# A two-layer backbone step on one core: the second layer's modulation vectors made at other places, the sums joined with x two groups earlier, some work moved off VectorE at layer edges

## The chip, the cores and the metric

One core of a Trainium2 chip runs the whole program. The time is the device time of one execution in microseconds; the figure for a kernel is the median of several executions. The kernel before took 3270.18 us, the median of 3 runs (3263.32 to 3278.54).

## The reference, cut to what matters

Two layers run over 1152 tokens (1024 latent, 128 context) of width 1024. Latent and context tokens have a conditioning vector each, so that every modulation vector exists in two columns.

```python
def ada_modulation(cond, w_mod, b_mod):
    m = (jax.nn.silu(cond) @ w_mod + b_mod)[..., None, :]
    return jnp.split(m, 6, axis=-1)

def trunk_layer(x, cond, p, rg_h0, hg_s0, ctx_k, ctx_v):
    sh1, sc1, g1, sh2, sc2, g2 = ada_modulation(cond, p['w_mod'], p['b_mod'])
    h = rms_norm(x, p['norm1']) * (1 + sc1) + sh1
    xa, ga, bq, bff, bfb, bi, bg, cq, ck, cv = jnp.split(h @ p['w_in'], split_points, axis=-1)
    ...   # three mixers: convolution and RG-LRU, HGRN2, attention
    mix = jnp.concatenate([out_a, out_b, out_c.reshape(bsz, t_len, D_C)], axis=-1) @ p['w_out']
    x = x + g1 * mix
    h2 = rms_norm(x, p['norm2']) * (1 + sc2) + sh2
    x = x + g2 * (jnp.square(jax.nn.relu(h2 @ p['w1'])) @ p['w2'])
```

A layer's modulation is 6 × 1024 values for each of the two conditionings: 48 tiles of 128 values, numbered j = 0 to 47 in the order sh1, sc1, g1, sh2, sc2, g2.

## The kernel before, in words

Features lie on partitions, tokens along the free axis: 8 tiles of 128 features by 1152 tokens. A layer passes through these stages, one after the other in TensorE's queue with some overlap: the input projections; the mixers, in which RG-LRU and HGRN2 (mostly VectorE) are woven with the remaining projections, and attention with the output projection; the first MLP product with w1; the second with w2. In the trace's order of time, the first layer's mixers run from about 117 to 790 us, its first MLP product from 800 to 1229, its second from 1235 to 1677; the second layer's mixers from 1758 to 2398, its MLP products from 2408 to 2833 and from 2838 to 3247.

All large matmuls are done in three passes on a high part and a low part of each operand. The high part is a rounded copy (ScalarE, L186), the low part the difference, made by GpSimd (`psub`, L189) or VectorE (`vsub`, L192). Which engine takes which of a weight's seven low parts is `lo_subs`, with the counts in `W2_SUBS`.

Both MLP products run by a scheme that needs seven products of operand sums in place of eight (`Line.products`, L1105): a product is one set of seven, with banks bA, bB, bC and bE of PSUM. It has 84 matmuls of 288 columns in the first MLP product (32 products) and 42 in the second (64 products: 8 groups of 8). Its results are taken off the banks by `c11`, `c22`, `c12`, `c21` on ScalarE and VectorE. In the first MLP product these results are hidden units; they and their sums and differences are prepared as operands of the second and stored to memory: `od` holds those with a high and a low part, `or` the raw sums. Their places on chip are `od_` (2 places) and `hx_` (3), cut out of `spare`, which in the first layer is the tile `sil` that held the conditioning.

In the second MLP product, each group of products loads its operands into a ring of 18 tiles (`R`, pools `tp0` and `tp1`) and adds its results to `rows` (L198). `combine` (L1819) joins two rows at a time with x: rows = rows × g2 + x, at the places in `MERGE`; groups after that add with g2 as a scalar (L210). In the last group the squares of finished rows are summed (`Sums`), and rms_rest turns the sums into the next norm's scale: st (matmul), rr (VectorE, GpSimd), dg (a copy on VectorE, L183), rb (matmul), rs (ScalarE).

`mod_tile` (L276) makes one tile j of the modulation: pieces of w_mod are loaded (`wm`) and multiplied and summed with the conditioning `sil` by VectorE (L286), once for each conditioning. In the first layer, tiles 16 to 47 of its own modulation are made in the mixers (`mods`, L1447), in pieces of 384, 384 and 256. In the second MLP product of the first layer tiles 0 to 39 of the second layer's modulation are made in whole tiles of 1024 on the ring `hr_`, and in the second layer's second MLP product tiles 40 to 47 (`MODS2`). Small rings: `sqt` has four tiles of 384, `xt` 24, `g_` 28.

The instructions of each engine are put in a fixed order by a scheduler when the program is built; `high_priority` moves a piece forward. All DMAs are issued from SP's queue, in order, each behind the waits of those before it.

## Time and profile before

| | |
|---|---|
| runs, median (lowest, highest) | 3270.18 us (3263.32, 3278.54) |
| profiled execution, device time | 3276.47 us |
| its span, first to last instruction | 3274.7 us |
| mean granted TensorE clock | 0.95 |
| busy: TensorE, VectorE, ScalarE, GpSimd | 90%, 73%, 50%, 48% |
| moved by DMA | 566 MB, 173 GB/s on average |

Engines are called PE (TensorE), DVE (VectorE), ACT (ScalarE), POOL (GpSimd) and SP in the rows. PEclk is the granted share of TensorE's clock: 1.00 is 2.4 GHz, 0.50 is 1.2 GHz, and a mean between them is a share of the stretch at either. A busy share is an average over a stretch, so rows of one stage are set beside rows of the same stage in the other layer.

### The profile page before, as it was taken

What the parts mean: (1) busy time and instruction counts of PE and PEld (TensorE: products, weight loads), DVE (VectorE), ACT (ScalarE), POOL (GpSimd) and SP (SyncE); (2) the same over time, 40 slices, a digit from 0 to 9 for tenths busy, and PEclk for the clock granted to TensorE, in tenths of its full rate; (3) what the DMA queues carried; (4) which work ended last, traced back from release to release, by engine and by line L of the source; (5) the groups of instructions that cost most, each with busy time, mean ns of one, the idle gap of its engine ahead of it and who ended that gap; (6) DMA issues with size and microseconds to landing.
All of it is one profiled execution on the core that took longest, in us unless ns stands there. A gap on an engine that the chain in (4) does not pass through costs nothing. (4 is left out here: it accounts for less than half of the span.)

```text
span 3274.7 us, 61327 instructions
## 1 busy us (share of the span) xinstructions
PE 2960.4 (90%) x21208; PEld 2815.3 (86%) x21208; DVE 2406.1 (73%) x5283; ACT 1641.4 (50%) x4079; POOL 1567.8 (48%) x1528
## 2 busy tenths in 40 slices
PE   7888998998889998988868999999987999899995
PEld 7878888798789998888858889988977999899994
DVE  8899974667885568998874677346779755777787
ACT  5543234565566666344454533345646566654443
POOL 4541132345676665554545311334556765654453
PEclk8989999999899998999979999999998999999997
DMA  7342447983455567675522102689634655855552
GB/s 270 91 108 87 132 121 224 283 269 103 158 176 185 177 212 279 216 245 198 181 94 74 58 29 80 183 239 293 220 127 148 194 179 181 281 204 173 185 194 68
DMA packets 391318, 566.48 MB, mean 173 GB/s; under 512 B 45920, under 2 KB 250848, under 8 KB 391008
## 3 DMA queue, kind: packets, MB, share of 16 engines
q1 hardware_dynamic: 391008, 562.57, 53.8%
q8 instruction: 167, 2.74, 0.4%
q14 instruction: 143, 1.17, 0.1%
HBM read 397.01 MB, written 165.42 MB: 172 GB/s over the span
## 5 line engine op out<-in xcount | busy, mean ns | idle before, releaser
L189 POOL TENSOR_TENSOR wl<-wr,wh 128x512 fp32r<-128x512 f32 x164 | 231.1, 1413 | 485.4 <-ACT wh L186 379.2
L189 POOL TENSOR_TENSOR wt<-wl,wt 128x256 fp32r<-128x256 f32 x276 | 258.0, 942 | 176.5 <-ACT wt L186 116.5
L1110 PE MATMUL bB<-R,wt 128*128 128x288 f32 x768 | 236.9, 309 | 63.7 <-ACT bB L186 40.8
L189 POOL TENSOR_TENSOR ws<-wl,ws 128x512 fp32r<-128x512 f32 x160 | 227.5, 1426 | 121.4 <-ACT ws L186 121.3
L421 PE MATMUL pj<-hh,wh 128*128 128x384 f32 x640 | 223.7, 354 | 27.0 <-ACT g L213 12.3
L1110 PE MATMUL bB<-t,ws 128*128 128x288 f32 x768 | 231.7, 302 | 18.0 <-DVE hr L198 9.6
L423 PE MATMUL pj<-hh,wl 128*128 128x384 f32 x640 | 225.1, 352 | 7.1 <-POOL wl L189 7.1
L1111 PE MATMUL bB<-R,wt 128*128 128x288 f32 x768 | 231.1, 301 | 0.0
L1112 PE MATMUL bB<-R,wt 128*128 128x288 f32 x768 | 230.0, 300 | 0.0
L1111 PE MATMUL bB<-t,ws 128*128 128x288 f32 x768 | 229.6, 299 | 0.0
L1112 PE MATMUL bB<-t,ws 128*128 128x288 f32 x768 | 229.2, 299 | 0.0
L422 PE MATMUL pj<-hh,wh 128*128 128x384 f32 x640 | 223.4, 350 | 0.0
L1110 PEld LDWEIGHTS bB<-R,wt 128*128 128x128 f32 x768 | 148.2, 193 | 74.2 <-ACT bB L186 48.3
L186 ACT CAST wt<-wl 128x256 fp32r<-128x256 f32 x288 | 115.9, 406 | 159.8 <-PE bB L1112 82.0
L421 PE MATMUL wo<-u,wh 128*128 128x288 f32 x512 | 160.1, 314 | 17.1 <-DVE x L210 13.4
L1110 PEld LDWEIGHTS bB<-t,ws 128*128 128x128 f32 x768 | 147.6, 192 | 22.0 <-DVE hr L198 11.4
L186 ACT CAST wh<-wr 128x512 fp32r<-128x512 f32 x164 | 101.1, 618 | 129.3 <-PE pj L422 65.2
L207 POOL TENSOR_SCALAR pl<-pl,rc 128x384 f32<-128x384 f32 x128 | 79.1, 618 | 176.5 <-DVE rc L952 83.9
L1110 PE MATMUL bA<-R,wt 128*128 128x288 f32 x512 | 156.0, 305 | 8.1 <-DVE row L210 5.8
L1112 PE MATMUL bA<-t,ws 128*128 128x288 f32 x512 | 155.4, 304 | 8.0 <-DVE ws L192 6.5
L1110 PE MATMUL bA<-t,ws 128*128 128x288 f32 x512 | 155.1, 303 | 4.3 <-ACT ws L186 2.3
L1111 PE MATMUL bA<-R,wt 128*128 128x288 f32 x512 | 154.6, 302 | 0.0
(363 smaller groups left out, 11364.9 us busy)
## 6 DMA issues: line engine op xcount, KB each, us to landing
wr<-in_w SPq DMA_DIRECT2D x304, 256.0 KB, 3.3
R<-od SPq DMA_DIRECT2D x96, 576.0 KB, 5.6
xb<-or SPq DMA_DIRECT2D x128, 288.0 KB, 4.2
wm<-in_w_mod SPq DMA_DIRECT2D x64, 512.0 KB, 5.6
od<-sil SPq DMA_DIRECT2D x96, 288.0 KB, 2.9
od<-pad SPq DMA_DIRECT2D x96, 288.0 KB, 3.1
wr<-in_w_in SPq DMA_DIRECT2D x104, 256.0 KB, 3.0
bi<-in_bias SPq DMA_DIRECT2D x96, 192.0 KB, 4.5
```

The source lines that it names most:

```text
L186: nc.scalar.copy(out=out, in_=in_)
L189: nc.gpsimd.tensor_tensor(out=out, in0=a, in1=b, op=ALU.subtract)
L207: nc.gpsimd.tensor_scalar(out=out, in0=a, scalar1=s1, scalar2=s2, op0=op0, op1=op1)
L421: mm(ps, lhsT=wh(k), rhs=ah(k), start=k == first, stop=False)
L422: mm(ps, lhsT=wh(k), rhs=al(k), start=False, stop=False)
L423: mm(ps, lhsT=wl(k), rhs=ah(k), start=False, stop=k == last)
L1110: mm(ps, lhsT=w[:, 0, ti(i)], rhs=t[:, 0], start=start and i == 0, stop=False, skip_group_check=True)
L1111: mm(ps, lhsT=w[:, 0, ti(i)], rhs=t[:, 1], start=False, stop=False, skip_group_check=True)
L1112: mm(ps, lhsT=w[:, 1, ti(i)], rhs=t[:, 0], start=False, stop=i == n - 1, skip_group_check=True)
```

## The change

- **Modulation.** Tiles 0 to 15 of the second layer's modulation are made in the first layer's first MLP product, over products 10 to 30 (`MLP_MODS`), in pieces on `sqt`; tiles 16 to 47 in the second layer's mixers, by the loop that the first layer has had. The second MLP products make none. For this, `sil` is loaded again in the first MLP product, and from product 8 on `od_` and `hx_` come from the rings `xr_` and `sqt`. `sil2` then stays until the second layer's mixers end; RG-LRU's weights `gw` and the gates `gel` change pools in that layer.
- **Joins.** `MERGE` names places two groups earlier, so the last two groups add with g2 as a scalar.
- **Operand ring.** The 18 tiles come from three pools of 4, 11 and 3 in turn, where they came from two of 7 and 11 with the first three turns skipped.
- **Less on VectorE at edges.** The squares of the second half's x are summed as each output tile is done (`late`), not after all; the scale's second step (`rms_turn`) is put in without the first step's priority. The first chunk's low parts of the second layer are made by ScalarE and GpSimd (`spare_vector`); the 64 context columns of the MLP's norm go from VectorE to ScalarE; in the last group of the second MLP product GpSimd makes all low parts of the weights.

```diff
-MODS2 = (2, 44)
+MLP_MODS = (10, 30)
...
-MERGE = (NG - 2, 2, 0), (NG - 2, 3, 0), (NG - 1, 0, 0), (NG - 1, 1, 0)
+MERGE = (NG - 3, 2, 0), (NG - 3, 3, 0), (NG - 2, 0, 0), (NG - 2, 1, 0)
...
-            vts(u, u, g[:, 1:2], sh[:, 1:2])
+            act(u, u, AF.Identity, scale=g[:, 1:2], bias=sh[:, 1:2])
...
-                gel[i][n] = (gl_ if l and n < 2 else xt)("gel")
+                gel[i][n] = (g_ if l and n < 2 else xt)("gel")
...
-        gw = [g_("gw")[:, :2 * P] for _ in range(4)]
+        gw = [(xt if l else g_)("gw")[:, :2 * P] for _ in range(4)]
...
-                mod_tile(0, j, piece)
+                mod_tile(l, j, piece)
...
-        left = iter(range(16, 48 if l == 0 else 16))
+        left = iter(range(16, 48))
...
                     dma(xmid[m][:, hs(q)], xn[m][q])
+                    if q:
+                        late.add([[(0, BLK, 0, u)] for u in blocks_of(xn[m][q])[:2]])
...
+        late = Sums(2)
...
-        sq = [block_sums(xn, b) for b in (2, 3)]
...
+        later = iter(range(16))
...
                     with tc.high_priority(URGE1):
-                        rs = [None, None] + [rms_rest(t, pa, BLK // 3) for t in sq]
+                        R = [rms_scale(t, pa, BLK // 3) for t in late.sq]
+                    rs = [None, None] + [rms_turn(t, pa, BLK // 3) for t in R]
+                    with tc.high_priority(URGE1):
...
+                if not last and n == MLP_MODS[0] - 2:
+
+                    od_, hx_ = repeat(lambda: xr_("od")), repeat(lambda: sqt("hx")[:, :BLK])
+                    for c in range(2):
+                        load_cond(c)
+                if not last:
+                    for e in take(later, steps(16, MLP_MODS, n - 1)):
+                        mod_tile(l + 1, e, sqt)
...
-        tp0 = phase(st0, "tp0", 7, T, "right")
+        tp0, tp1 = phase(st0, "tp0", 4, T, "right"), phase(st0, "tp1", 3, T, "right")
...
-        tp1 = phase(st1, "tp1", 11, T, "right")
-
-        turn = cycle([tp0] * 7 + [tp1] * 11)
-        run_out(take(turn, 3))
+        tp2 = phase(st1, "tp2", 11, T, "right")
+
+        turn = cycle([tp0] * 4 + [tp2] * 11 + [tp1] * 3)
...
-        later = iter([(1, j) for j in (range(40, 48) if last else range(40))])
-        n_later, n = (8 if last else 40), 0
...
-                          lambda i: lo_subs(W2_SUBS[0] if i < W2_SUBS[1] else W2_SUBS[2]))
+                          lambda i: lo_subs(W2_SUBS[0] if i < W2_SUBS[1] else W2_SUBS[2] if i < len(order[0]) + 4 * (NG - 2) else 0))
...
-                elif g < NG - 1:
+                elif g < NG - 2:
                     vtt(t, ps, t, ALU.add)
...
-                    for a in take(later, steps(n_later, MODS2, n)):
-                        mod_tile(*a, hr_, junk1)
...
-                        modulate(l + 1, False, xs, 0, ht, rs[0])
+                        modulate(l + 1, False, xs, 0, ht, rs[0], True)
```

How the order changes at three places. VectorE in the first layer at the start of the first MLP product, where sq are the sums of squares of the second half, rr and dg steps of the scale, wl and ws weights, hr, s and sil hidden units. Before:

```order
L198 TENSOR_TENSOR sq<-sq 128x288
L198 TENSOR_TENSOR hr<-bB,s_10260 128x288
L204 TENSOR_SCALAR rr<-st 96x6
L198 TENSOR_TENSOR sq<-sq 128x288
L192 TENSOR_TENSOR wl<-wr,wl 128x512
L192 TENSOR_TENSOR ws<-wr,ws 128x512
L198 TENSOR_TENSOR sq<-sq 128x288
L198 TENSOR_TENSOR wl<-wr 128x512
L198 TENSOR_TENSOR sq<-sq 128x288
L198 TENSOR_TENSOR sil<-bC,s_10260 128x288
L183 COPY dg<-rr 96x384
L198 TENSOR_TENSOR sq<-sq 128x288
```

and now:

```order
L198 TENSOR_TENSOR sq<-sq 128x288
L192 TENSOR_TENSOR wl<-wl,wr 128x512
L192 TENSOR_TENSOR wl<-wr 128x512
L198 TENSOR_TENSOR hr<-bB,s_10260 128x288
L192 TENSOR_TENSOR wl<-wr,wl 128x512
L204 TENSOR_SCALAR rr<-st 96x6
L192 TENSOR_TENSOR ws<-wr,ws 128x512
L204 TENSOR_SCALAR rr<-st 96x6
L198 TENSOR_TENSOR wl<-wr 128x512
L183 COPY dg<-rr 96x384
```

The sums of squares, seven of which stood behind the last update of x (the rows show five), have moved ahead, but for one; rr and dg follow each other more closely.

VectorE in the middle of the first layer's first MLP product, from one product's sum out of bB to the next instructions. wm are pieces of w_mod, ma and mod the accumulated sums, hr, hx and sil hidden units. Before:

```order
L198 TENSOR_TENSOR hr<-bB,s_11409 128x288
L192 TENSOR_TENSOR wl<-wl,wr 128x512
L198 TENSOR_TENSOR sil<-bC,s_11409 128x288
L210 SCALAR_TENSOR_TENSOR sil<-sil 128x288
L192 TENSOR_TENSOR hr<-sil,hr 128x288
L192 TENSOR_TENSOR sil<-hr,sil 128x288
L192 TENSOR_TENSOR wl<-wr 128x512
L192 TENSOR_TENSOR hr<-hr 128x288
L192 TENSOR_TENSOR ws<-wr,ws 128x512
L192 TENSOR_TENSOR sil<-sil,hr 128x288
L198 TENSOR_TENSOR hr<-bB,s_11564 128x288
```

and now:

```order
L198 TENSOR_TENSOR hr<-bB,s_12151 128x288
L286 ISA junk,ma<-wm,sil,ma 128x384
L286 ISA ma 128x1
L286 ISA junk,mod_117<-wm,sil,ma 128x256
L286 ISA mod_117 128x1
L286 ISA junk,mod_117<-wm,sil,ma 128x256
L286 ISA mod_117 128x1
L198 TENSOR_TENSOR hx<-bC,s_12151 128x288
L210 SCALAR_TENSOR_TENSOR hx<-hx 128x288
L192 TENSOR_TENSOR wl<-wr,wl 128x512
L192 TENSOR_TENSOR hr<-hx,hr 128x288
```

Dot products stand between the sum out of bB and the one out of bC; hx has the place that sil had.

SP's queue at the same stage, a stretch of about one product. in_w is w1, or and od the prepared operands in memory. Before:

```order
L216 DMA od_9797<-sil 256x1x288
L216 DMA or_9798<-sil 128x288
L216 DMA od_9797<-sil 256x1x288
L216 DMA wr<-in_w 128x512
L216 DMA od_9797<-sil 256x1x288
L216 DMA or_9798<-hr 128x288
L216 DMA or_9798<-sil 128x288
L216 DMA or_9798<-hr 128x288
L216 DMA od_9797<-sil 256x1x288
L216 DMA or_9798<-sil 128x288
L216 DMA wr<-in_w 128x512
```

and now:

```order
L216 DMA od_9797<-od 256x1x288
L216 DMA or_9798<-hr 128x288
L216 DMA or_9798<-hx 128x288
L216 DMA wm<-in_w_mod 128x384
L216 DMA or_9798<-hr 128x288
L216 DMA wm<-in_w_mod 128x384
L216 DMA wm<-in_w_mod 128x256
L216 DMA od_9797<-od 256x1x288
L216 DMA or_9798<-hx 128x288
L216 DMA wr<-in_w 128x512
L216 DMA od_9797<-od 256x1x288 x2
```

Three loads of w_mod stand between the stores of a product and the next weight.

## Rows read from the trace of the kernel before

**Rows 1.** The page's first part: busy us, share, instructions by engine.

```profile
PE 2960.4 (90%) x21208; PEld 2815.3 (86%) x21208; DVE 2406.1 (73%) x5283; ACT 1641.4 (50%) x4079; POOL 1567.8 (48%) x1528
```

**Rows 2.** Busy time by stretch: from:to length, engines (instructions), PEclk, DMA, GB/s.

```profile
117.00:790.00 673.00, 610.48 (x4499) 554.34 (x4500) 520.62 (x1503) 303.70 (x817) 233.72 (x283) 0.95 0.55 160
1758.00:2398.00 640.00, 605.26 (x4505) 549.57 (x4504) 391.73 (x1106) 306.29 (x818) 228.91 (x283) 0.97 0.49 143
800.00:1006.00 206.00, 176.81 (x1202) 172.15 (x1202) 165.54 (x238) 112.52 (x263) 134.84 (x102) 0.91 0.52 168
2408.00:2610.00 202.00, 173.94 (x1205) 169.54 (x1204) 165.60 (x238) 113.15 (x264) 132.11 (x102) 0.92 0.53 172
1006.00:1184.00 178.00, 178.00 (x1344) 178.00 (x1343) 99.78 (x149) 107.93 (x249) 114.08 (x100) 1.00 0.56 181
1263.00:1578.00 315.00, 285.24 (x2019) 278.89 (x2018) 294.85 (x568) 135.40 (x340) 163.68 (x146) 0.96 0.66 224
2867.00:3146.00 279.00, 272.68 (x2018) 270.38 (x2017) 208.50 (x424) 136.06 (x340) 137.45 (x146) 0.99 0.57 192
1578.00:1633.00 55.00, 48.53 (x340) 46.76 (x339) 51.44 (x105) 25.52 (x64) 30.75 (x31) 0.97 0.48 158
3146.00:3204.00 58.00, 50.24 (x337) 49.00 (x335) 51.52 (x106) 26.36 (x67) 29.90 (x30) 0.91 0.45 150
1633.00:1694.00 61.00, 32.97 (x205) 30.40 (x204) 54.37 (x128) 30.99 (x81) 17.49 (x17) 0.77 0.29 104
```

**Rows 3.** The dot products of line 286 alone, by stretch.

```profile
117.00:790.00 673.00, 131.67 (x382) 0.95 0.55 160
1263.00:1578.00 315.00, 114.89 (x160) 0.96 0.66 224
2867.00:3146.00 279.00, 22.56 (x32) 0.99 0.57 192
```

**Rows 4.** VectorE's groups, 1598 to 1658 us: busy, mean ns, idle before.

```profile
L210 DVE SCALAR_TENSOR_TENSOR row<-row,mod,xm 128x1024 f32<-128x1024 f32 x4 | 5.6, 1398 | 0.0
...
L210 DVE SCALAR_TENSOR_TENSOR row<-bB,mod,row 128x224 f32<-128x224 f32 x6 | 2.6, 437 | 0.0
...
L210 DVE SCALAR_TENSOR_TENSOR row<-row,mod,xm 128x128 f32<-128x128 f32 x4 | 2.3, 573 | 0.0
...
L198 DVE TENSOR_TENSOR row<-bB,row 128x288 f32<-128x288 f32 x4 | 1.8, 442 | 0.0
L210 DVE SCALAR_TENSOR_TENSOR row<-bB,mod,row 128x64 f32<-128x64 f32 x6 | 1.6, 269 | 0.0
```

**Rows 5.** Subtractions by operation: least/median/most ns, first and last start, forms.

```profile
L189 POOL TENSOR_TENSOR wt<-wr,wt x35: 727/747/1782, 1235.3 to 1647.4; 128x256 fp32r<-128x256 f32 x35
...
L192 DVE TENSOR_TENSOR wt<-wr,wt x72: 406/414/1653, 1235.6 to 1655.3; 128x256 fp32r<-128x256 f32 x72
...
L189 POOL TENSOR_TENSOR hh<-nt,hh x8: 993/1018/1337, 20.2 to 60.4; 128x384 fp32r<-128x384 f32 x8
```

**Rows 6.** VectorE's groups at the edge between the layers, 1633 to 1694.

```profile
L210 DVE SCALAR_TENSOR_TENSOR hh<-nt,mod,hh 128x384 fp32r<-128x384 f32 x8 | 4.6, 609 | 0.0
```

**Rows 7.** VectorE in order of time, 846 to 853 us: start, length.

```profile
848.07 3.50 DVE L198 TENSOR_TENSOR sq<-sq 128x288 f32<-128x288 f32 x1
...
851.85 0.53 DVE L183 COPY dg<-rr 96x384 f32<-96x384 f32 x1
```

**Rows 8.** TensorE's groups, 790 to 960 us.

```profile
L348 PE MATMUL rb<-ident,dg 96*128 96x96 f32 x12 | 2.4, 354 | 6.3 <-DVE dg L183 6.3
```

**Rows 9.** Line 204 on VectorE, 860 to 930 us: least/median/most ns.

```profile
L204 DVE TENSOR_SCALAR xb<-xb,am,mod x8: 298/366/792, 868.8 to 902.0; 128x64 f32<-128x64 f32 x8
```

**Rows 10.** DMA issues of the whole span: count, KB each, median us to landing.

```profile
or<-sil SPq DMA_DIRECT2D x64, 144.0 KB, 2.3
...
wm<-in_w_mod SPq DMA_DIRECT2D x32, 128.0 KB, 2.3
```

**Rows 11.** VectorE's groups, 117 to 540 us, the costliest.

```profile
L286 DVE CUSTOM_DVE_ANT_0 junk<-wm,sil,ma 128x384 bf16<-128x384 f32 x64 | 47.2, 738 | 3.6 <-DMA wm<-in_w_mod 2.8
```

More of the change, by code (lines that the diff above doesn't have):

```diff
@@ L1 @@
 from contextlib import ExitStack, nullcontext
-from itertools import cycle
+from itertools import cycle, repeat
 import concourse.bass as bass
@@ L274, in build, with mod_tile @@
     am = [C.tile([P, 16, 2], F32, name=f"am{l}") for l in range(DEPTH)]
-    def mod_tile(l, j, piece, junk=junk):
+    def mod_tile(l, j, piece):
         acc = [pcol(l, "bm", j)] * 2
@@ L1639, in build @@
         oraw = tc.dram_tile([NG, 2, len(SUMS), P, 2 * BLK], F32, name=f"or{l}")
-        od_ = cycle([spare[:, i * 2 * BLK:(i + 1) * 2 * BLK] for i in range(2)])
-        hx_ = cycle([spare[:, i * BLK:(i + 1) * BLK] for i in range(4, 7)])
+        od_ = cycle([lambda i=i: spare[:, i * 2 * BLK:(i + 1) * 2 * BLK] for i in range(2)])
+        hx_ = cycle([lambda i=i: spare[:, i * BLK:(i + 1) * BLK] for i in range(4, 7)])
         st = ExitStack()
@@ L1684, in part @@
             def part(p, t):
-                o = next(od_).bitcast(F32R).rearrange("p (j m) -> p j m", j=2)
+                o = next(od_)().bitcast(F32R).rearrange("p (j m) -> p j m", j=2)
                 acopy(o[:, 0], t)
@@ L1715, in c1 @@
             def c1(r, ps):
-                t = next(hx_) if r else ft("hr")[:, :BLK]
+                t = next(hx_)() if r else ft("hr")[:, :BLK]
                 act(t, ps, AF.Relu)
@@ L1721, in c2 @@
             def c2(r, ps):
-                t = ft("hr")[:, :BLK] if r else next(hx_)
+                t = ft("hr")[:, :BLK] if r else next(hx_)()
                 vtt(t, ps, on.s5, ALU.add)
@@ L1759, in build @@
             sil_st.close()
-        sil_st = ExitStack()
-        sil = phase(sil_st, "sil2", 1, 2 * DM)("sil").rearrange("p (c d) -> p c d", c=2)
+        if not last:
+            sil_st = ExitStack()
+            sil = phase(sil_st, "sil2", 1, 2 * DM)("sil").rearrange("p (c d) -> p c d", c=2)
+            for c in range(2):
+                load_cond(c)
         h_st, row_st, st0, st1 = (ExitStack() for _ in range(4))
@@ L1781, in build @@
             run_out(group_operands(s))
-        for c in range(2):
-            load_cond(c)
-        later = iter([(1, j) for j in (range(40, 48) if last else range(40))])
-        n_later, n = (8 if last else 40), 0
         rows = [row_("row") for _ in range(KD)]
```

11 lines of the change are left out of this document (3 added, 8 removed).

## The prediction

> **What bounds the kernel now.** Busy time by engine [rows 1]: TensorE 90%, VectorE 73%. Both are averages over stages with different limits, so next I read the table by stage [rows 2], its rows in pairs: the same stage of the first and the second layer. The two layers run the same matmuls. They differ in where the modulation vectors are made: by 32 tiles in the first layer's mixers and none in the second's, by 40 tiles in the first layer's second MLP product and 8 in the second's. Each pair is therefore a measurement of what this change moves, and most of the sum is read from pairs.
>
> The scale is the steady part of the first MLP product: 1344 matmuls in 178.0 us, TensorE never idle, 132.4 ns each [rows 2]. At that pace 2018 matmuls take 267.2 us. The second MLP product takes 315.0 us for them in the first layer and 279.0 us in the second: 48 us lost against 12. VectorE is busy 294.9 of 315.0 us in the first and 208.5 of 279.0 us in the second, and the dot products of the modulation (L286) make 114.9 and 22.6 us of that [rows 3]. There VectorE is the bound and TensorE waits for its evacuations. The same pair for the mixers: 673 us with 131.7 us of dot products, 640 us with none, at equal matmuls (4499 and 4505). All of VectorE's difference, 520.6 less 391.7, is dot products. At the layer edges VectorE is full too: 54.4 of 61 us while TensorE does 33 us of work [rows 2].
>
> **The change part by part.**
>
> *Tiles out of the second MLP products.* 40 tiles go in the first layer. What is left is the second layer's stretch, less what its 8 tiles cost: 36.0 us are given back surely by the pair, 48 at most (full pace). I take 38. In the second layer 8 tiles go: 0 to 12 us, I take 2, since 22.6 us of work there fell into 70 us of free VectorE.
>
> *32 tiles into the second layer's mixers.* That stage becomes the first layer's: 640 to 673 us, +33. Below, 0, if they fit into the 248 us in which VectorE is free there; above, by the price that the second MLP product's pair gives (36.0 us lost for 92.3 us of dot products, 0.39 each), 131.7 × 0.39 = 51. I take 33, the row that shows the very same work.
>
> *16 tiles into the first layer's first MLP products.* One tile in 384-wide pieces costs VectorE 131.7 / 32 = 4.1 us, so 16 cost 66 us, over 20 products of 84 matmuls (11.1 us each, 222 us). VectorE is busy 99.8 of 178.0 us there, 56%; with the tiles it comes to 86%. Below 0 (98 us are free), above 66 × 0.39 = 26. I take +8, nearer to zero because a product here has twice the matmuls per evacuation. In the order, three of a tile's six dot products stand before a product's sum from bB and three between it and the sum from bC, so a piece that lands late holds hr<-bB up, and TensorE, which goes on in the bank that this reads, waits for it.
>
> *The joins with x two groups earlier.* Eight joins per layer, 1398 + 573 ns each [rows 4], 15.8 us of VectorE, leave the two last groups; with them 14 low-part subtractions per layer go to GpSimd (14 × 414 ns = 5.8 us off VectorE, 14 × 747 ns = 10.5 us on GpSimd, which is busy 30.8 of 55 us there) [rows 2, 5]. The stretch that they leave takes 55.0 us for 340 matmuls in the first layer and 58.0 us for 337 in the second: 10.0 and 13.4 us over full pace. But the joins land three products into a stretch with about 2 us free per product, and the next-to-last group's sums are now two-operand with a scalar: 16 of 442 ns become 437 + 269 [rows 4], 4 us more. So half of the gain is paid back earlier: −5 per layer, bounds −13 and +6.
>
> *Edge between the layers.* Eight operations of 609 ns, 4.9 us, leave VectorE [rows 6] for ScalarE and GpSimd (8 × 1018 ns [rows 5]; GpSimd is busy 17.5 of 61 us). −4, bounds 0 and −10. At the program's end only the subtractions help: −2.
>
> *Sums of squares taken along.* At the first MLP product's start TensorE waits 6.3 us for the copy dg [rows 8], which starts at 851.85 because two-operand sums stand before it, one of 3.50 us [rows 7]. In the new order one sum is left behind the last update of x, where seven were, and three instructions stand between the first rr and its dg, not seven. The wait goes. Next late are the second half's operands and the weights, which VectorE and GpSimd make together; eight operations of 366 ns [rows 9] go from VectorE to ScalarE there. 206 and 202 us for 1202 and 1205 matmuls, at a granted clock of 0.91 and 0.92 [rows 2]: a shorter wait also gives back some of the stretch at 1.2 GHz. −8 per layer; below −15, above −2 (the turn stands only 12 places nearer to its sums in TensorE's order, 1.6 us).
>
> *The operand ring.* Four, eleven and three tiles in turn give the same 18 places in the same order as seven and eleven with three skipped; only an address shifts where the scratch tile goes. 0.
>
> Sum: −38 − 2 + 33 + 8 − 10 − 4 − 2 − 16 = −31 us. The profiled execution took 3276.5 us (span 3274.7), which gives 3245.5; the median of the runs is 3270.2, 6.3 lower, so I predict 3239.
>
> **A rule that speaks against it.** VectorE's 256-wide subtractions have a minimum of 406 ns and a maximum of 1653, GpSimd's 727 and 1782 [rows 5]: each is often stretched by the other. The Trainium skill, SBUF — State Buffer, section "Who interferes with whom", says that a VectorE instruction with two SBUF inputs and a GpSimd instruction that reads SBUF exclude each other, so that the later one stands still. By that rule, moving a 406 ns subtraction to an engine that needs 727 ns takes nothing from VectorE's stretch but adds to it, as long as VectorE's own work is two-operand. The maxima agree with it; sums out of PSUM stay at 442 ns [rows 4], as it says for one SBUF input. It makes a rival below.
>
> **The rivals.**
> 1. *The tiles cost as much where they go.* VectorE at 75% loses 12 of 279 us, at 94% 48 of 315 [rows 2]; at 86% in the first MLP product that is some 10% by interpolation, 22 us and not 8; and the joins only move their loss, 0 for −10. For it: the pairs. Against: TensorE is never idle in the steady first MLP product. Time 3239 + 14 + 10 = 3263, no change.
> 2. *Slower: the four-slot ring and SP's queue.* Two hidden tiles of each product and the pieces of w_mod now share four slots. The third piece can be asked for only when the store of the hidden tile four allocations before has landed (2.3 us), then needs 2.3 us itself [rows 10], 4.6 us per tile; SP waits in order, so the od stores and weight loads behind it wait as well (the order shows them there), and ScalarE, which needs od's slot, and so TensorE. A product has some 1.6 us of VectorE to spare (14% of 11.1). If the chain isn't hidden in 20 products: 20 × (4.6 − 1.6) = 60 us; 3239 + 60 − 8 = 3291. It decides from about 1.6 us of wait per product. Against: the period is 11.1 us, and in the first layer's mixers, where 22 of the 32 tiles came through a ring of four, 64 dot products had VectorE wait 2.8 us for them in all [rows 11]. The Trainium skill, DMA: Bandwidth & Descriptors, "Anatomy of one DMA — SWDGE (gpsimd) path", says that any wait for a semaphore is made by the issuing sequencer before dispatch; by that one blocked load does hold all behind it.
> 3. *The lock.* The 28 low-part subtractions and 8 of the modulation given to GpSimd relieve nothing, so joins and edge give half: 3239 + 8 + 5 = 3252.
>
> **Numbers.** Forecast 0.55 (3222 to 3256, from −48 for the first term, 0 to +20 for the first MLP and −13 to 0 for joins); rival 1 0.22; rival 3 0.12; rival 2 0.11. About 0.5% (16 us) is what a measurement can tell from no change: faster lies under 3254, slower over 3286. Faster: most of the forecast, half of rival 3, a fifth of rival 1, 0.62. Same: the rest of these and a part of rival 2, 0.28. Slower 0.10. The range takes rival 1 whole and the lower bounds in part: 3208 to 3278.
>
> **What would show it.** The second layer's mixers at about 673 us with 130 us of dot products; both layers' second MLP stretch of 2018 matmuls near 277 us with none; no wait of several us before rb at the first MLP's start; the first MLP's products 10 to 30 of the first layer at 11.1 to 11.6 us. It is wrong if those products are over 13 us with ScalarE or VectorE waiting for DMA (rival 2), or if the mixers lose clearly more than 40 us.

## The result, and the profile after

The changed kernel took 3308.64 us (median of 4 runs, 3306.69 to 3312.97) where the kernel before took 3267.09 us in the same comparison: ratio 1.0117, 95% interval 1.0100 to 1.0134. By the ratio it is slower by some 38 us; 3239 us was forecast, and the range ended at 3278. The profiled execution of the changed kernel has a span of 3304.9 us, 30.2 more than before's 3274.7, and this difference can be told stage by stage. A row below runs from the first matmul of one product to the first of another (products numbered in the order of time), in one profiled execution of each kernel.

| stretch | before | changed | difference | forecast |
|---|---|---|---|---|
| start to the first layer's first MLP product | 800.0 | 796.7 | −3.3 | 0 |
| first layer, first MLP, products 0 to 8 | 158.8 | 154.2 | −4.6 | −8 |
| the same, product 8 to the end | 270.1 | 324.4 | **+54.3** | **+8** |
| gap and first four products of the second MLP | 34.2 | 41.3 | +7.1 | 0 |
| second MLP, products 4 to 52 | 315.0 | 274.8 | −40.2 | −38, and joins |
| products 52 to the end | 99.4 | 91.2 | −8.2 | joins (−5 with the row above) |
| from there to the second layer's first MLP | 730.7 | 769.4 | +38.7 | +33 − 4 |
| second layer, first MLP, products 0 to 12 | 201.6 | 198.9 | −2.7 | −8 |
| second MLP, products 4 to 52 | 279.0 | 275.4 | −3.6 | −2, and joins |
| products 52 to the end | 101.3 | 92.8 | −8.5 | joins |
| all else | | | +1.2 | −2 |

One row carries the miss: +54.3 us where +8 was forecast. The page's first part, against [rows 1], shows VectorE with more work, 2478.7 for 2406.1 us:

```profile
PE 2963.3 (90%) x21208; PEld 2822.5 (85%) x21208; DVE 2478.7 (75%) x5631; ACT 1646.8 (50%) x4119; POOL 1570.9 (48%) x1564
```

Most of that is dot products, which cost more in pieces than as whole tiles of 1024. Against [rows 3], 130.5 + 61.8 + 131.2 us for 131.7 + 114.9 + 22.6:

```profile
117.00:787.00 670.00, 130.50 (x382) 0.96 0.55 160
796.70:1005.10 208.40, 1.81 (x3) 0.90 0.54 173
1005.10:1215.20 210.10, 47.61 (x154) 0.95 0.57 181
1215.20:1275.30 60.10, 12.38 (x36) 0.94 0.76 245
1766.00:2440.00 674.00, 131.18 (x380) 0.96 0.55 159
```

Busy time by stretch, columns as in [rows 2]: first the steady part of the first layer's first MLP (16 products) and its last four; then the same 16 products in the second layer, where no tiles are made; the second MLP, products 4 to 52, of both layers; and a stretch that holds the second layer's mixers.

```profile
1005.10:1215.20 210.10, 189.77 (x1347) 187.44 (x1346) 167.01 (x306) 103.23 (x249) 119.82 (x100) 0.95 0.57 181
1215.20:1275.30 60.10, 49.13 (x337) 47.69 (x336) 49.83 (x91) 29.17 (x68) 28.67 (x24) 0.94 0.76 245
...
2650.90:2829.20 178.30, 178.30 (x1347) 178.30 (x1346) 99.87 (x150) 108.12 (x250) 114.01 (x101) 1.00 0.56 182
...
1316.60:1591.50 274.90, 270.33 (x2019) 268.71 (x2018) 194.69 (x408) 134.75 (x336) 133.93 (x145) 1.00 0.57 193
2909.30:3184.70 275.40, 271.57 (x2018) 270.16 (x2017) 194.52 (x408) 134.64 (x336) 134.05 (x145) 0.99 0.57 193
...
1766.00:2440.00 674.00, 611.27 (x4495) 554.84 (x4494) 515.67 (x1488) 307.22 (x825) 234.72 (x280) 0.96 0.55 159
```

The first and third rows are the same 1347 matmuls: 210.1 against 178.3 us, 13.1 us a product for 11.1. TensorE's own busy time is 189.8 against 178.3, as the granted clock is 0.95 and not 1.00, so 11.5 of the 31.8 us are matmuls run in part at 1.2 GHz; the other 20.3 are waits. What it waits for is in the waits of that stretch (total us, times, longest):

```profile
DVE junk L286 <- DMA wm<-in_w_mod: 32.8, 13, 5.2
PEld bB L1110 <- DVE hr L198: 22.7, 10, 3.7
PE bB L1110 <- DVE hr L198: 20.3, 10, 3.5
```

TensorE waits for VectorE to take bank bB, and VectorE waits 32.8 us for pieces of w_mod. One such case in order of time (start, length, and in brackets the idle time ahead), VectorE first:

```profile
1042.69 1.05 DVE L192 TENSOR_TENSOR hr<-hr 128x288 f32<-128x288 f32 x1
1047.61 0.62 DVE L286 CUSTOM_DVE_ANT_0 junk<-wm,sil,par 128x384 bf16<-128x384 f32 x1 [3.86 <-DMA wm<-in_w_mod]
...
1049.72 0.45 DVE L198 TENSOR_TENSOR hr<-bB,s 128x288 f32<-128x288 f32 x1
```

then SP's queue:

```profile
1043.77 0.32 SPq L216 DMA_DIRECT2D or<-hr  x1
1044.15 1.46 SPq L216 DMA_DIRECT2D wm<-in_w_mod  x3
```

and TensorE:

```profile
1046.99 0.29 PE L1112 MATMUL bB<-t,ws 128*128 128x288 f32 x1
1050.23 0.40 PE L1110 MATMUL bB<-t,ws 128*128 128x288 f32 x1 [2.94 <-DVE hr L198]
```

VectorE ends a difference of hidden units at 1043.74; SP, which held the store of it at its head, issues the store at 1043.77 and only then the three loads; the first piece is there 3.5 us later. VectorE has stood for 3.86 us by then, makes its dot products, and takes bB at 1049.72. TensorE goes on at 1050.23. So VectorE waits for a load that was queued behind its own last result. This is the rule in the stretch and not one case: before 10 of its 11 waits of over 0.2 us, the instruction that SP was last held at was a store of a hidden unit that VectorE had just made (27.2 of 32.4 us). At the loads of pieces themselves SP was held once, for 0.6 us, until a store had landed. The Trainium skill, DMA: Bandwidth & Descriptors, "Anatomy of one DMA — SWDGE (gpsimd) path", states that a wait for a semaphore is made by the issuing sequencer before dispatch. SP's rows agree: the store was issued 0.03 us after VectorE's result was there, and the loads behind it.

### The profile page after: what moved, and what is told of

Same layout as the page of the kernel before. It is cut to its first block, busy times and chain, and to the rows that moved or that the text cites. A ratio compares the mean times of both kernels' runs of the same rounds, so it can differ in the third digit from the quotient of the medians.

```text
span 3304.9 us, 61952 instructions
## 1 busy us (share of the span) xinstructions
PE 2963.3 (90%) x21208; PEld 2822.5 (85%) x21208; DVE 2478.7 (75%) x5631; ACT 1646.8 (50%) x4119; POOL 1570.9 (48%) x1564
## 5 line engine op out<-in xcount | busy, mean ns | idle before, releaser
L189 POOL TENSOR_TENSOR wt<-wl,wt 128x256 fp32r<-128x256 f32 x276 | 230.7, 841 | 162.8 <-ACT wt L186 108.6
L1110 PE MATMUL bB<-t,ws 128*128 128x288 f32 x768 | 236.4, 308 | 49.2 <-DVE hr L198 40.3
L1110 PE MATMUL bB<-R,wt 128*128 128x288 f32 x768 | 232.1, 302 | 31.5 <-DVE row L210 17.8
L1111 PE MATMUL bB<-t,ws 128*128 128x288 f32 x768 | 234.7, 306 | 8.1 <-DVE t L192 8.1
L1112 PE MATMUL bB<-t,ws 128*128 128x288 f32 x768 | 234.5, 305 | 0.0
L1111 PE MATMUL bB<-R,wt 128*128 128x288 f32 x768 | 228.7, 298 | 0.0
L1112 PE MATMUL bB<-R,wt 128*128 128x288 f32 x768 | 228.0, 297 | 0.0
L286 DVE CUSTOM_DVE_ANT_0 junk<-wm,sil,ma 128x384 bf16<-128x384 f32 (+1 forms) x320 | 212.2, 663 | 9.1 <-DMA wm<-in_w_mod 4.4
L1110 PEld LDWEIGHTS bB<-R,wt 128*128 128x128 f32 x768 | 146.4, 191 | 36.6 <-DVE row L210 18.9
L1110 PE MATMUL bA<-R,wt 128*128 128x288 f32 x512 | 154.9, 303 | 21.9 <-DVE row L210 9.9
L189 POOL TENSOR_TENSOR wt<-wr,wt 128x256 fp32r<-128x256 f32 x100 | 81.8, 820 | 171.4 <-PE bA L1112 63.0
L1112 PE MATMUL bA<-t,ws 128*128 128x288 f32 x512 | 156.5, 306 | 5.4 <-POOL ws L189 5.4
```

The lines of the kernel that those rows point to most:

```text
L189: nc.gpsimd.tensor_tensor(out=out, in0=a, in1=b, op=ALU.subtract)
L286: nc.vector.tensor_tensor_reduce(out=junk[:, :w], in0=r[:, :w], in1=sil[:, c, k0:k0 + w], scale=1.0, scalar=acc[c], op0=ALU.mult, op1=ALU. ...
L1110: mm(ps, lhsT=w[:, 0, ti(i)], rhs=t[:, 0], start=start and i == 0, stop=False, skip_group_check=True)
L1111: mm(ps, lhsT=w[:, 0, ti(i)], rhs=t[:, 1], start=False, stop=False, skip_group_check=True)
L1112: mm(ps, lhsT=w[:, 1, ti(i)], rhs=t[:, 0], start=False, stop=i == n - 1, skip_group_check=True)
```

## The experiments

Each ratio is to the kernel before, run on the same chip, with its 95% interval; the changed kernel has 1.0117. Stretches are from one profiled execution each, and those differ: the stretch of 324.4 us (first layer, first MLP, product 8 to the end), with its code unchanged, came to 320.6 in another kernel. The steady products are products 12 to 28 of that stage.

**Without the loads.**

```diff
+            if load:
+                r = piece("wm")
+                dma(r[:, :w], I["w_mod"][l, j][:, k0:k0 + w])
...
+                if not load:
+                    r = sil[:, 1 - c, k0:k0 + w]
...
-                        mod_tile(l + 1, e, sqt)
+                        mod_tile(l + 1, e, sqt, False)
```

> The changed kernel with the 16 tiles of the first layer's first MLP product kept, but their first operand is the other conditioning (on chip) instead of a loaded piece: the loads, and so the values of these 16 tiles, are left out. The stretch looked at runs from product 8 of that stage to its end: 270.2 us in the kernel before, 324.4 in the changed one. Theory A (VectorE waits for pieces that SP asks for late, behind the stores of the same product): the waits of 38.6 us go and the stretch comes to 272 to 285 us, the kernel to about 3265. Theory B (VectorE's 66 us of additional work are the price, wherever the pieces come from): the stretch stays at 315 to 325 us, the kernel at about 3305.

The ratio is 1.0065 (1.0045 to 1.0086), and the stretch took 315.0 us. The figure is at the lower end of theory B's, but it decides nothing, for the edit changed a second thing. With no load and no place to wait for, the scheduler drew the dot products forward, two tiles to a product. Products 8 to 20 took 15.1 us each with VectorE busy 84%, and then came 11.1 us each:

```profile
944.30:1124.90 180.60, 149.66 (x1010) 147.28 (x1009) 152.62 (x313) 83.10 (x193) 97.49 (x79) 0.91 0.47 148
1124.90:1214.00 89.10, 89.10 (x674) 89.10 (x673) 50.28 (x78) 54.15 (x126) 53.88 (x49) 1.00 0.58 182
```

**A ring of their own for the pieces.**

```diff
-W1_RING, W2_RING = (7, 7), 11
+W1_RING, W2_RING = (6, 7), 11
...
+        wm_ = None if last else phase(tq_st, "wm1", 3, NW, "left")
...
-                        mod_tile(l + 1, e, sqt)
+                        mod_tile(l + 1, e, wm_)
```

> The changed kernel with the pieces of w_mod in that stage on a ring of their own of three tiles, so that a tile's loads wait only for the dot products of the tile before and stand in SP's order nearly a product ahead; the ring of w1 goes from seven to six places to make room. Theory A: the wait for the pieces falls from 38.6 us to under 8, the stretch from product 8 to the end (324.4 us) to 275 to 290 us, the kernel to 3260 to 3275. Theory B: stretch 315 to 325. A third outcome, that six places of w1 cost by themselves, would show as TensorE waiting for ws in products before the tiles too, and in no wait for wm.

The ratio is 1.0063 (1.0046 to 1.0079), and the stretch took 318.4 us, a figure of theory B's. The waits for pieces fell from 38.6 to 9.3 us, nearly as theory A had it, but the tiles crowded as above (products 8 to 20 took 15.0 us each), and the stretch stayed long. The run is inconclusive for the same reason.

**Priority for the loads.**

```diff
-            dma(r[:, :w], I["w_mod"][l, j][:, k0:k0 + w])
+            with tc.high_priority(100) if 0 < j < 16 and l else nullcontext():
+                dma(r[:, :w], I["w_mod"][l, j][:, k0:k0 + w])
```

> The changed kernel with priority for these loads alone, same ring: in SP's order the three pieces move ahead of one store (from behind a store that waits for VectorE's difference to ahead of it), no further, since the ring's places hold them. Theory A: each exposed wait of about 3.6 us shrinks by the 0.6 to 1 us that the store waited, 13 to 16 times: stretch 324 to 308 to 316 us, kernel 3293 to 3301. Theory B: no change, 3305 to 3310.

The ratio is 1.0097 (1.0075 to 1.0119), and the stretch took 321.5 us. VectorE still waits 34.4 us for pieces, 38.6 in the changed kernel. One store's place is not enough: SP was then last held at another instruction that VectorE releases, a weight load that waits for `wl` or the store of the other hidden unit (20.9 of the 29.3 us of waits in the steady products). The figure is theory B's, no change: the difference is within what executions scatter. It doesn't speak against late pieces, since they stayed nearly as late.

**16 tiles in the second MLP product.** The 16 tiles go to the first layer's second MLP, products 2 to 44, with pieces on the four-slot ring, and none stay in its first; the hidden units keep their old places.

```diff
+                    n += 1
+                    for e in take(later, steps(16, MODS2, n)):
+                        mod_tile(l + 1, e, sqt)
```

> The changed kernel with the 16 tiles in the first layer's second MLP product (products 2 to 44, pieces on the four-slot ring, no other user there) and none in its first; hidden units on the places that they had before. First MLP product back to 425 to 430 us under every theory. Theory A (cost depends on how the pieces arrive and on free time of VectorE, which has 80 of 275 us there): products 4 to 52 go from 274.9 to 278 to 285 us, the kernel to 3257 to 3266. Theory B (a tile costs about 1 us wherever it goes, 40 us for 40 tiles): 290 us, the kernel at 3270.

The ratio is 1.0000 (0.9987 to 1.0013). The first MLP is back at 270.1 us; the second took 304.3 for 274.8, 29.5 us for 16 tiles and more than either theory had. Again they had crowded, into the products up to 28 (first row, VectorE 92% busy), and the rest ran at full pace (second row):

```profile
1252.40:1412.60 160.20, 142.89 (x1011) 140.68 (x1010) 147.17 (x382) 73.55 (x183) 70.96 (x73) 0.95 0.62 203
1412.60:1502.80 90.20, 90.08 (x674) 89.60 (x674) 67.17 (x140) 42.58 (x104) 43.85 (x49) 1.00 0.57 191
```

So most of the next kernels hold each tile to its product, by one column of a result of that time, times zero, added to the bias that the first dot products start from:

```diff
+        if pace is not None:
+            b = tiny("pb", 1)
+            pts(b, pace[:, 0:1], 0.0, acc[0])
+            acc = [b] * 2
```

**Paced, own ring.**

> As the run with a ring of its own for the pieces (six places for w1), but each tile's first dot products also need a hidden unit of the product before, by a one-column GpSimd operation, so that the tiles keep one product's distance as in the changed kernel (1 to 8 dot products per product) and don't crowd two into one. Looked at: product 8 of the first layer's first MLP to its end, 270.1 us before, 324.4 changed, 318.4 with the own ring alone. Theory A (the late pieces are the price: VectorE's 167 busy us of 210 there would fit, its 33 us of waiting for pieces don't): 275 to 287 us, kernel some 40 us faster than the changed one (ratio to before 0.998 to 1.002). Theory B (at such a busy share VectorE's order alone makes TensorE wait, pieces or not): 297 to 318 us, ratio 1.005 to 1.011.

**Paced, no loads.**

> The changed kernel (seven places for w1) with the same pace, and the first operand of the 16 tiles' dot products taken from the conditioning on chip, so that no piece is loaded there and the values of these tiles are left out. It differs from the run before it only in that nothing is loaded and the ring of w1 is whole. Theory A: 272 to 284 us for the stretch. Theory B: as in that run, 297 to 318 us. If this one is fast and the other slow, the loads cost in another way than by a wait of VectorE (SP's queue, memory traffic).

**Paced, and else as changed** (the control for both).

> The changed kernel (four shared places, seven of w1, loads as they are) with the pace of the paced runs and nothing else: the control for them. Its dot products stand in the same order as in the paced run without loads. If the late pieces make the difference between 324 us and the paced runs' 295 to 297 (product 8 of the first MLP to its end): 315 to 326 us with some 30 us of VectorE waiting for pieces, ratio 1.009 to 1.013. If it was the pace: 293 to 300 us.

The ratios are 1.0011 (0.9998 to 1.0023) with the own ring, 1.0050 (1.0030 to 1.0070) without loads and 1.0104 (1.0087 to 1.0120) for the control. The stretches from product 8 to the end took 294.8, 296.7 and 320.1 us. The control is as it should be if the late pieces count. The other two lie beyond theory A's 287 and 284 us and about where theory B begins, 297: the pieces are some half of the loss, and what is left needs other causes. The windows of the 16 steady products show the parts. First the own ring:

```profile
1000.30:1185.30 185.00, 180.41 (x1347) 178.59 (x1346) 176.12 (x305) 101.72 (x249) 131.81 (x114) 1.00 0.65 208
```

without loads:

```profile
1001.60:1192.90 191.30, 181.41 (x1346) 178.66 (x1345) 180.17 (x307) 101.49 (x249) 129.69 (x113) 1.00 0.51 166
```

the control, and two of its waits:

```profile
1000.20:1209.90 209.70, 189.41 (x1346) 187.88 (x1345) 175.28 (x305) 103.74 (x249) 127.50 (x113) 0.93 0.57 182
```

```profile
DVE junk L290 <- DMA wm<-in_w_mod: 22.6, 12, 3.8
...
PE bB L1114 <- DVE hr L198: 20.3, 6, 5.6
```

These are three kernels with the same VectorE work, 175 to 180 us, in almost the same order. Where pieces come in time or aren't loaded, the products take 185 and 191 us at a granted clock of 1.00, and VectorE has no wait for pieces; where they come late, 210 at 0.93, though VectorE's busy time is the least. So the late pieces are worth 18 to 25 of the 32 us in these products, their part in the clock included. The other 7 to 13 remain without them, with VectorE 94 to 95% busy; that they are the price of its fullness is argued from that share. The profiled executions of the first two are at the low end of their runs, 3.5 and 12.0 us under the medians, so the 18 above all may be too large; by the ratios the whole kernels gain 30 and 18 us on the control. The own ring changes several things at once: the places that a load waits for, its position in SP's order, and one place less for w1. In the changed kernel SP was held at the stores ahead of the loads and not at the loads, which speaks for the position; but the scheduler may have put the loads there because of the shared places, and that was not separated.

**8 and 8.** Eight tiles in the first MLP product (paced, own ring, `steps(8, MLP_MODS, n - 1)`), eight in the second.

> The changed kernel with 8 tiles in the first layer's first MLP product (own ring of three, w1 on six places, paced) and 8 in its second (four-slot ring, paced). With all 16 in one place the paced tiles cost 25 us in the first product (270.1 to 294.8, products 8 to the end, VectorE 95% busy) and 15 us in the second (274.9 to 290.2). Theory C (a tile's price grows with how full VectorE is): 8 tiles leave VectorE at some 75% in the first and some 85% in the second, so 2 to 6 us each, 272 to 276 and 277 to 281 us; ratio to before 0.993 to 0.996. Theory B (price per tile constant, 1.6 and 0.95 us): 282.5 and 282.5 us, ratio 0.998 to 1.000.

The ratio is 0.9981 (0.9972 to 0.9990). The steady products run at full pace with their share of the eight tiles in them, VectorE busy 83%, and the second MLP takes 278.6 us, +3.8:

```profile
1005.50:1183.70 178.20, 178.20 (x1346) 178.20 (x1345) 148.73 (x222) 104.62 (x248) 125.26 (x108) 1.00 0.61 199
```

At this count the tiles cost 0 there where sixteen, paced, cost 7: theory C, and the second MLP is in its range too. But the whole stretch took 283.4 us, not 272 to 276; this and the ratio are theory B's figures, met for another reason than a constant price. Products 8 to 12 (53.6 for 47.2) and the last four (51.5 for 44.7) are long in this kernel as in the changed one (54.2 and 60.1).

**The conditioning loaded early, used late.** Of products 8 to 12 in the changed kernel, two waits, and a part of what ScalarE runs there (op, count, least, median and most ns, first and last start):

```profile
ACT L213 <- DMA sil<-in_cond: 7.7, 1, 7.7
...
PE bB L1110 <- ACT bB L186: 6.5, 1, 6.5
```

```profile
L213 ACT ACTIVATE sil<-sil x2: 1044/1050/1056, 965.5 to 967.3; 128x1024 f32<-128x1024 f32 x2
L213 ACT ACT_TABLE_LOAD  x1: 1283/1283/1283, 964.3 to 964.3; - x1
```

```diff
-                        load_cond(c)
+                        load_cond(c, True)
+                if not last and n == MLP_MODS[0]:
+                    for c in range(2):
+                        late_cond(c, latest[0])
```

The same was done at the start of the second MLP, and the tiles' ranges begin at products 11 and 4 in place of 10 and 2.

> The kernel with 8 tiles in each MLP product, with one edit: the conditioning is loaded as it was (at product 8 of the first MLP and at the start of the second), but ScalarE's Silu on it stands three products behind the load in the first MLP and four in the second, held back until a result of that time is there. In the run before it ScalarE waits 6.4 us for that load at about 962 us and TensorE 4.9 us for a copy behind it on ScalarE, and 4.7 us once more at the first product's end. Looked at: products 8 to 12 (53.6 us; 47.1 before) and 28 to the end (51.5; 44.8 before). Theory D (these 13 us, which don't grow with the tiles, are ScalarE standing in its queue for the load): 47 to 49 and 45 to 48 us, ratio 0.994 to 0.997. Theory E (they are the hidden units' new places, rings of two and four shared with the pieces): 52 to 54 and 50 to 52, ratio 0.997 to 0.999.

> The kernel with all 16 tiles paced in the second MLP product, but with the hidden units of its first product moved at product 8 to the places of the changed kernel (two shared, four shared), and no conditioning loaded there. Theory D: products 8 to 12, 12 to 28 and 28 to the end as in the kernel before (47.1, 178.2, 44.8 us). Theory E: 8 to 12 at 51 to 54, the end at 50 to 52 us.

Products 8 to 12 took 46.9 us with the split: ScalarE's wait at the head of its queue was those 6.7 us, theory D. The price is not a fixed one: two kernels with the same reload (no loads paced, and the old places of the joins) took 48.8 us there, with TensorE waiting 2.6 and 2.7 us behind ScalarE. The end did not follow (53.3). The other kernel didn't test what it was to test at the start: with the old place of the conditioning free, the scheduler drew the load meant for the next stage forward to product 8, where ScalarE waited 6.5 us for it (51.7 us). Its end, with the new places and neither tiles nor a load, took 45.9 for 44.7: the places cost some 1 us there. The 7 us at the end with eight tiles stay open. The split kernel as a whole has 0.9993 (0.9981 to 1.0006), no better than without and outside both theories' ranges, since its second MLP product came to 288.8 us for 278.6. Why is not known.

**Paced in the second MLP product.** As with the 16 tiles there before, each now held by a result of the product before.

> The changed kernel with the 16 tiles in the first layer's second MLP product, as in the earlier run that did so, where they crowded into products 4 to 28 and took the stretch of products 4 to 52 from 274.9 to 304.3 us; now each tile needs a result of the product before, which spreads them over products 2 to 40. Theory C (crowding: VectorE was full for 100 us and idle later): 280 to 290 us, ratio to before 0.991 to 0.996, faster than both kernels. Theory B (each tile costs its work, some 1.8 us, wherever it stands): 300 to 305 us, ratio 0.999 to 1.001.

**The ratio is 0.9972 (0.9962 to 0.9983), the fastest kernel here**: 9 us faster than the kernel before, 47 than the changed one by the ratios. The 16 tiles cost 15.4 us, half of what they cost crowded; 290.2 us for products 4 to 52 lies just past the far end of theory C, and the ratio between the two theories.

**The mixers' tiles spread.** The kernel just above, with 16 of HGRN's 22 tiles moved in both layers to the attention and the output projection, paced by attention's results.

```diff
-        n = sum(MODS[1:3])
+        n = 6
...
+            if i >= 8:
+                run_out(mods(1, sqt))
```

> The paced kernel with 16 tiles in the first layer's second MLP product, and with the mixers' 32 tiles spread anew in both layers: 10 in RG-LRU as before, 6 in HGRN in place of 22, 16 in attention and the output projection, each held back until an attention result of that step is there. In the changed kernel VectorE is busy 235 of 249 us in the second layer's HGRN (86 us of it dot products) and 123 of 232 us in the attention, where there are none. Theory C (a tile costs what VectorE lacks in the stretch where it stands): HGRN 249 to 222 to 230 us, the attention 232 to 232 to 242, the end of the second MLP product to the start of the next layer's first from 769 to 778 us to 745 to 755; the same in the first layer; kernel 3225 to 3245 on the scale of before's 3267 to 3276, ratio 0.984 to 0.991. Theory B (a tile costs its work wherever it stands): no change against the run before, ratio 0.996 to 0.999.

The ratio is 1.0011 (0.9999 to 1.0023), a loss against 0.9972, and outside both theories. In the second layer matmul 2500 of the stretch came 18.9 us earlier, and all of it was gone at the end (778.5 for 775.6 us). In the first layer it went further: the first MLP product starts at 808.4 us for 795.5, which is the whole loss between the two profiled executions (12.8 us). The tiles had crowded once more. Below are three rows of 50 us; those from 2050 to 2200 have no dot product:

```profile
2150.00:2200.00 50.00, 47.27 (x317) 40.38 (x315) 22.82 (x65) 25.45 (x80) 17.38 (x27) 0.94 0.80 225
2200.00:2250.00 50.00, 46.62 (x369) 38.29 (x368) 44.92 (x160) 23.50 (x78) 24.01 (x35) 1.00 0.96 292
2250.00:2300.00 50.00, 40.27 (x288) 32.54 (x286) 42.54 (x154) 22.90 (x84) 20.52 (x34) 0.90 0.98 298
```

VectorE is 85 to 90% busy in the two rows with dot products, but the DMA engines are 96 to 98% busy there as well, and between 2200 and 2350 us VectorE waits 9.9 us for pieces. What the crowding cost and what the pieces' traffic in a stage that moves much already was not separated.

**The old places of the joins.**

```diff
-MERGE = (NG - 3, 2, 0), (NG - 3, 3, 0), (NG - 2, 0, 0), (NG - 2, 1, 0)
+MERGE = (NG - 2, 2, 0), (NG - 2, 3, 0), (NG - 1, 0, 0), (NG - 1, 1, 0)
...
-                elif g < NG - 2:
+                elif g < NG - 1:
```

> The changed kernel with the joins with x at the places that they had before (last group but one and last). Looked at: products 52 to the end of the second MLP product, 91.2 and 92.8 us in the two layers of the changed kernel, 99.4 and 101.3 before, and products 4 to 52. If the joins' place is what those 8 us come from, they go back to 97 to 101 us while 4 to 52 get 2 to 5 us shorter; if the low parts given to GpSimd did it, they stay at 91 to 94.

There is one execution, of 3308.07 us. The low parts stay with GpSimd. Products 52 to the end went back to 100.5 and 99.3 us, products 4 to 52 fell to 269.9 and 270.4. So the joins' new place takes 9.3 and 6.5 us out of the end and puts 4.9 and 5.0 back earlier: −4.4 and −1.5. With unchanged code products 4 to 52 of the second layer spread from 275.4 to 279.1 us over the kernels here, so the −1.5 is not clear of the scatter.

**The old sums of squares.**

```diff
+        sq = [block_sums(xn, b) for b in (2, 3)]
...
-                        R = [rms_scale(t, pa, BLK // 3) for t in late.sq]
-                    rs = [None, None] + [rms_turn(t, pa, BLK // 3) for t in R]
+                        rs = [None, None] + [rms_rest(t, pa, BLK // 3) for t in sq]
```

> The changed kernel with the sums of squares of the second half made after all output tiles, and rr and dg in one prioritised step, as before. Looked at: products 0 to 8 of the first layer's first MLP (158.8 us before, 154.2 to 156.7 in the changed kernel and its variants) and 0 to 12 of the second's (201.6; 197.8 to 200.8). If the sums taken along are the gain there: 158 to 160 and 201 to 203 us, and TensorE waits 6 us before rb again. If not, 154 to 157 and 198 to 201.

There is one execution, of 3327.07 us. The wait of 6.3 us before rb is back in both layers, where the changed kernel has 3.0. The second layer's products 0 to 12 took 206.1 us, 7.2 longer; the first layer's 0 to 8 took 155.5, within the others' scatter. So the gain is shown for the second layer only.

## Why the prediction was wrong, step by step

- **The step that failed: "I take +8, nearer to zero because a product here has twice the matmuls per evacuation", for the 16 tiles in the first MLP product.** It measured +54.3, beyond its upper bound of 26. The same paragraph named the mechanism, a piece that lands late holds hr<-bB and with it TensorE, and put no price on it: the working counted VectorE's work and a share of it, not when each piece arrives. By the runs, 18 to 25 us are late pieces in the steady part. Another 7 to 13 are left there with the pieces in time or not loaded. VectorE is then 95% busy and not 86%: with the own ring its dot products take 67.7 us in those products, where 4.1 us a tile gives 53, and its other work 108 for 99.8. Some 7 are the reload of the conditioning, at products 8 to 12, which was not in the sum at all. And 15 are the last four products, where tiles, the next load and the next stage's first operands meet; TensorE waits 8.6 us there for VectorE's sum out of bB, but this part was not tested. The sign of being wrong that the prediction named, products of over 13 us with VectorE waiting for DMA, is what came: 13.1 us.
- **Rival 2 named the place and the queue, and was given 0.11, but its chain is not the one seen.** It had a load that waits for its place in the four-slot ring and holds the stores behind it; the trace has a store that waits for VectorE and holds the loads behind it, and SP stands 0.6 us in the 16 products for the landing of a store of `or`. That its 60 us for this stage are near 54 is luck: some 18 to 25 of the 54 are late pieces. It was argued down by the period of 11.1 us and by the 2.8 us of waits in the mixers [rows 11]. Neither row speaks of this: a load's place in the queue counts. In the steady products SP was last held at a store of VectorE's hidden units ahead of 32 of 37 loads; in the first layer's mixers of the kernel before, for 66 of 87 loads, at the load itself. The order in the part on the change showed this, `or` ahead of `wm`, and was not followed to its end: the store's data come from VectorE's last difference, a few instructions ahead of the dot product.
- **The tiles out of the second MLP products: right.** −40.2 for −38 with the joins' payback in it, −45.1 without (269.9 for 315.0), within the bound of 48 (269.9 us is from the one execution with the old places of the joins). Second layer −3.6, and −8.6 without the joins, for −2.
- **The mixers: right in kind, +33 taken, some 37 measured** (38.7 with the edge, of which about 2 by the first 40 matmuls of the layer; the prediction's own window has 674.0 us for 640.0). Other kernels here had 768 to 779 us for that stretch. The loss is where VectorE is full. HGRN in the second layer, the kernel before (first row) and the changed one:

```profile
1852.90:2070.90 218.00, 211.13 (x1702) 191.98 (x1701) 164.99 (x493) 76.89 (x191) 41.10 (x45) 0.98 0.19 56
```

```profile
1858.60:2108.00 249.40, 222.92 (x1701) 206.01 (x1700) 234.90 (x729) 76.27 (x189) 53.56 (x54) 0.95 0.40 111
```

- **The joins: right in the first layer, −4.4 for −5; −1.5 in the second.** Rival 3, that the low parts given to GpSimd relieve nothing, fits: with the joins at their old places and the low parts on GpSimd, products 52 to the end took 100.5 and 99.3 us, 99.4 and 101.3 in the kernel before, so by one execution the low parts lost 1.1 us there and gained 2.0. Joins and edge together gave some 4 of their 14 us (its own price, 8 + 5 us, is more than the half that it names). That the engines' lock is the cause is not shown. The prediction read the rows of these subtractions as "often stretched"; their medians of 414 and 747 ns, close to the least of 406 and 727, say that most are not.
- **The first MLP's start: half the size,** −4.6 and −2.7 for −8 each. The wait before rb went from 6.3 [rows 8] to 3.0 us, not to none. In the first layer the gain is not clear of the scatter.
- **The edge: wrong sign, small,** about +2 for −4.
- **A cost that was not in the sum, with the hidden units' new places.** The second MLP's first four products and the gap ahead cost 7.1 us in the first layer, −0.3 in the second. ScalarE's first copy to a row waits for the last stores of the hidden units' new place, and TensorE for it:

```profile
PE bA L1110 <- ACT row L186: 5.7, 1, 5.7
ACT row L186 <- DMA od<-od: 4.2, 1, 4.2
```

  The operand ring, taken at 0, is not the cause: with the same ring and the hidden units at their old places (16 tiles in the second MLP, crowded and paced) these products and the gap took 34.0 and 33.9 us, and with the new places and no tile in the first MLP 40.9, where the same wait is back, 4.9 us on ScalarE and on TensorE.

  The kernels that have a ring of their own for the pieces and six places for w1 keep the new places and took 33.2 to 35.9 us, so the places alone don't decide it; the rest is open.

## What to carry to other kernels

Free time on an engine is not a price of zero for work moved there. What counts is when its input lands: look up which stores stand ahead of its load in the queue, and whether one of them waits for the very engine that will wait for the load. A scheduler that fills an idle engine draws moved work together; a dependency on a result of the time at which the work should run keeps it spread. In the second MLP sixteen tiles cost 29.5 us crowded and 15.4 spread, and in the steady products of the first, spread and with pieces in time, 7 us for sixteen and nothing for half as many. And count the set-up: the reload of a shared operand stood at the head of an engine's queue and cost 6.7 us in the kernel with eight tiles, about as much as sixteen tiles with pieces in time cost in the steady products.

## What the runs showed of the hardware that was not expected

- A wait of TensorE can cost more than itself. In the 16 steady products of the changed kernel 20.3 us of waits came with 11.5 us of slower matmuls (granted clock 0.95, a mean of 2.4 and 1.2 GHz); the paced kernels with the own ring and without loads, with 4.6 and 9.9 us between their matmuls, stayed at 1.00.
- Some of VectorE's instructions with two operands on chip got longer. In the 16 steady products of the changed kernel (count, busy us, mean ns, idle before):

```profile
L192 DVE TENSOR_TENSOR hr<-hx,hr 128x288 f32<-128x288 f32 x16 | 20.4, 1276 | 0.3
...
L192 DVE TENSOR_TENSOR hr<-hr 128x288 f32<-128x288 f32 x16 | 15.7, 980 | 1.2 <-DVE hx L192 0.5
L192 DVE TENSOR_TENSOR hx<-hr,hx 128x288 f32<-128x288 f32 x16 | 15.2, 952 | 1.1
...
L198 DVE TENSOR_TENSOR hr<-bB,s 128x288 f32<-128x288 f32 x16 | 7.2, 452 | 0.0
```

and in the kernel before, the same four operations in the same products:

```profile
L192 DVE TENSOR_TENSOR hr<-sil,hr 128x288 f32<-128x288 f32 x16 | 15.1, 945 | 0.6
L192 DVE TENSOR_TENSOR sil<-hr,sil 128x288 f32<-128x288 f32 x16 | 15.1, 943 | 1.1
...
L198 DVE TENSOR_TENSOR hr<-bB,s 128x288 f32<-128x288 f32 x16 | 7.3, 458 | 14.7 <-PE bB L1112 14.7
...
L192 DVE TENSOR_TENSOR hr<-hr 128x288 f32<-128x288 f32 x16 | 7.3, 455 | 0.8
```

  The sums out of PSUM did not change (452 for 458 ns). Of the operations on chip two grew, by 331 and 525 ns, one did not (952 for 943), and the fourth got shorter (635 for 791). So they are not all affected alike, and the landing of pieces is not needed for it: in the paced kernel without loads the one that went from 455 to 980 ns still takes 885. The Trainium skill, SBUF — State Buffer, "Who interferes with whom", gives a cause that would do this: a VectorE instruction with two inputs on chip and a GpSimd instruction that reads there exclude each other. No run here isolates it.
- Silu on the conditioning brought a load of ScalarE's table with it, 1.28 us, in the middle of a stage.
